# Four reorderings in a one-core decoder layer: query and key tiles by weight unit, the first branch's banks, the block sums, and the turns of the last rows

## The chip, the core and the metric

The kernel runs on one core of one Trainium2 chip. The metric is the time on the device in microseconds (us) of one execution; "the time" of a kernel is the median of its runs, while the profile and the trace come from one further, profiled execution. The engines are called by their names in the profile: PE (TensorE, with its weight loads apart as PEld), DVE (VectorE), ACT (ScalarE), POOL (GpSimd) and SP (SyncE, which issues most DMAs).

## The reference

One layer of a decoder, for 1024 tokens of width 1024, in float32:

```
xn   = rms_norm(x)
proj = xn @ w_in          # q, six key/value parts, 24 gates, conv in, memory q, 3 merge gates
A = sparse attention: compressed blocks, top-16 selected blocks, window of 512, each gated
B = GLU -> depthwise conv (31) -> layer_norm -> silu
C = attention over 256 memory tokens
merged = sig(g0) * (A @ w_nsa_out) + sig(g1) * (B @ w_conv_out) + sig(g2) * (C @ w_mem_out)
h   = x + merged @ w_out
out = h + (silu(hn @ w_gate) * (hn @ w_up)) @ w_down,   hn = rms_norm(h), d_ff = 2816
```

## The kernel before

**Products.** Each float32 operand is split in a high and a low part (`split`, L142: an ACT cast makes the high part at L143, a subtraction on DVE or POOL at L136 makes the low one). A product is three matmuls: high by high, high by low, low by high (`mm3`, L169; the matmuls are those of L162). A weight tile of 512 input rows and 256 columns is a *unit* (`unit`, L275); a product over 1024 input rows needs two units, u = 0 and u = 1, with four steps k of 128 rows each. `tok_proj` (L311) makes a tile of 256 tokens by 256 columns, token tile by token tile, and in each over all eight k, so over both units.

**Banks.** Results are summed in eight PSUM banks. Seven have the names ps0, ps1 and ps2 (three, three and one of them) and are taken in a fixed rotation by `bank`; with `at` a caller names the group. The eighth, pf, belongs to the *filler*; `fbank` takes it, and `anybank` takes it at every eighth call.

**Order.** The program text isn't the order of the engines' instructions. A scheduler lays each engine's instructions out ahead of time by priorities (the place in the text, plus an addition for work marked `low`) and by its own estimate of when operands are ready; `tc.add_manual_dep` ties one instruction behind another. On the chip each engine then runs its list strictly in order. Work marked `low(FILL)` is the filler (L825 to L839): the merge gates, 24 weight tiles with two halves each, so 48 products of 24 matmuls of 128x512. Each is summed in pf, copied by ACT to a tile fz (L838) and sent to memory (zd). It fills TensorE where the main work waits; all but the first 12 weight tiles are also tied along the attention, step by step.

**The stages.**
- To 346 us: norms and turns of x, the convolution and memory branches up to their projections, compressed keys.
- 346 to 371: the last query tiles (L603 to L614): eight token tiles of 280 columns, one after the other, each over both units; behind each, ACT copies, sigmoid and squares and a sum on DVE.
- 371 to 388: the LayerNorm of the convolution branch (L636 to L650): two sums over channels on TensorE, subtractions on DVE (L641), squares on ACT (L643).
- 388 to 456: keys and values (L660 to L684). For each of two weight pairs s, four tiles of 256 tokens; a finished key tile is normed, split and turned (`keys`, L668).
- 456 to 880: attention, along which the filler runs.
- 880 to 977: the three branches' output projections (L891 to L933): loop n_ over branches, dp over pairs of channel tiles, d_ and half inside; one tile is 12 matmuls. The gate comes back from zd, ACT makes its sigmoid (L903), and DVE multiplies it with the product: for the first branch directly into the sum `acc` (L914), for the others to a tile (L916) that is then added (POOL for the second, DVE at L917 for the third).
- 977 to 1062: h = x + merged @ w_out by seven block products (`out_product`, L1045, matmuls at L1052) of sums and differences of blocks of `merged`; four of these block sums for each j are made in place by `a_sums` (L883), called in the loop of the third branch at dp > 1. The sum of h is L1059, its squares L1061.
- 1040 to 1096: norm and turn of h in four groups of 256 rows. `scaled_h` (L980) takes the root (ACT, L154) and its reciprocal (DVE) and scales the rows (DVE, L986); `norm_h` (L989) turns them on TensorE (L1002) into four banks, splits them, and for the seven-product feed-forward part keeps copies (L1016) and differences. Between the turns of the last two groups stands `plain(0, 0)` (L965): the gate product and the up product of the first 128 columns, 24 matmuls each, with a Silu on ACT (L968) and a product on DVE (L970).
- From 1096: feed-forward and down projection, then the output.

Of the kernel before, what the change touches and what calls it, by code (L numbers as in the profile page):

```python
# [17 lines left out]
P = 128  # L18
# [15 lines left out]
ORDER = mybir.DependencyInfo(mybir.DependencyClass.NoSync, mybir.DependencyReason.DATA)  # L34
N_EARLY = 12
WB, LAG, SPREAD = 6, 4, 97
TAP_LEAD = 24
# [4 lines left out]
def hybrid_layer_kernel(  # L42
# [252 lines left out]
    def row_units(w, c0, alloc=wslab, eng=None, ready=None):  # L295
        return [unit(w[u * 512:(u + 1) * 512, c0:c0 + 256].rearrange("(k p) c -> p k c", p=P), [4, 256], alloc, eng,
                     ready=ready) for u in range(2)]

    def chan_proj(w, half, act=xn, n=P, alloc=bank):
# [292 lines left out]
    for u in range(2):  # L592
# [8 lines left out]
        ws.append(w)  # L601
    sums.append(small(NT * 4))
    for t in range(NT):  # L603
        half, a = t // 4, (t % 4) * P
        o = bank([WCOLS])
        for k in range(KT):
            w = ws[k // 4]
            mm3(o, xn(0, k, half, a, a + P), xn(1, k, half, a, a + P), w[:, 0, k % 4], w[:, 1, k % 4], k == 0,
                k == KT - 1)
# [4 lines left out]
        nc.vector.tensor_reduce(sums[-1][:, 4 * t:4 * t + 4], q.rearrange("p (h d) -> p h d", h=4), axis=AX.X, op=OP.add)  # L614
# [47 lines left out]
    for s, K, V in ((0, KS, VS), (1, KW, VW)):  # L662
# [8 lines left out]

        last = None
        for tp in range(4):
            v = tok_proj(ws, tp).rearrange("p t (a g d) -> p t a g d", a=2, g=2)
            kn = t2([2, 2, 64])
# [149 lines left out]
    with low(FILL):  # L825
        for n_ in range(3 * KT):
# [3 lines left out]
            for h_ in range(2):  # L830
# [7 lines left out]
                nc.scalar.copy(z, ps)  # L838
                nc.sync.dma_start(zd[b_, d_, :, h_ * 512:(h_ + 1) * 512], z)  # L839


# [40 lines left out]

    def a_sums(j):  # L883
        plus = nc.vector.tensor_tensor
        a11, a12, a21, a22 = (merged(th, kh, j) for th in range(2) for kh in range(2))
        plus(a22, a21, a22, op=OP.add)
        sub(nc.vector, a21, a11, a21)
        sub(nc.vector, a11, a22, a11)
        sub(nc.vector, a12, a12, a11)

    branches = ((1, ud, w_conv_out), (2, md, w_mem_out), (0, od, w_nsa_out))  # L891
    nxt = [unit(ud[k], [S], alloc=slab) for k in range(4)]
    for n_, (br, src, wt) in enumerate(branches):
        ins = nxt
        for dp in (range(4) if n_ < 2 else (0, 2, 1, 3)):
# [3 lines left out]
            for d_ in (2 * dp, 2 * dp + 1):  # L899
# [4 lines left out]
                for half in range(2):  # L904
                    z = zz[:, half * 512:(half + 1) * 512]
                    ps = anybank([512])
                    for k in range(4):
                        i_ = ins[k]
                        mm3(ps, w[:, 0, k, wc:wc + P], w[:, 1, k, wc:wc + P],
                            i_[:, 0, half * 512:(half + 1) * 512], i_[:, 1, half * 512:(half + 1) * 512],  # L910
                            k == 0, k == 3)
                    a = acc[dp][:, d_ % 2, half * 512:(half + 1) * 512]
# [5 lines left out]
                    if n_ == 2 and (half, dp // 2) != (1, 0):  # L918
# [4 lines left out]
                        split(m[:, 0, d_ % 2, :], m[:, 1, d_ % 2, :], a)  # L923
            if n_ == 2 and dp > 1:
                a_sums(dp - 2)
            if n_ == 2 and dp == 1:
# [37 lines left out]

    def plain(f, half, w):  # L965
        pg = chan_proj(w[0], half, alloc=anybank)
        s_ = t2([512])
        nc.scalar.activation(s_, pg, AF.Silu)  # L968
        pu = chan_proj(w[1], half, alloc=anybank)
        nc.vector.tensor_tensor(s_, pu, s_, op=OP.mult)  # L970
        emit_act(f, half, s_)
        return s_

    T = [[None] * 2 for _ in range(4)]
    raw, held = [None, None], [[], []]

# [12 lines left out]
    def norm_h(tp, js, at=None):  # L989
# [7 lines left out]
        def turned(kp):  # L997
            b = fbank([2, 256]) if at and kp == 3 else bank([2, 256], at=at and at[kp])
            for kk in range(2):
                k = 2 * kp + kk  # L1000
                for tt in range(2):
                    nc.tensor.transpose(b[:, kk, tt * P:(tt + 1) * P], js[tt][:, k * P:(k + 1) * P], ident)  # L1002
            split(XN[half][kp][:, 0, :, c], XN[half][kp][:, 1, :, c], b)
# [9 lines left out]
        if half == 0:  # L1013
            raw[0], raw[1] = [sb_fz() for _ in range(2)], t4([2, 2, 256])
            for kp in range(4):
                nc.scalar.copy(raw[0][kp] if kp < 2 else raw[1][:, kp - 2], turned(kp))  # L1016
            return
# [93 lines left out]
    finish(2, s_3, w_7, 1)  # L1111
    norm_h(0, js, (1, 1, 1))
    js = scaled_h(1)
    finish(2, left[1, 1], w_4, 0)
    nc.sync.dma_start(hd[2], H[2])
    js2 = scaled_h(2)
    norm_h(1, js, (1, 1, 1))
    w0 = gate_up(0)
    finish(3, s_3, w_7, 1)
    norm_h(2, js2, (0, 0, 1))  # L1120
    finish(3, left[1, 1], w_4, 0)
    nc.sync.dma_start(hd[3], H[3])
    js3 = scaled_h(3)
    for f_ in held[0]:
        f_()
    held[0].clear()
    a0 = plain(0, 0, w0)
    norm_h(3, js3)
    left_low(0, a0, plain(0, 1, w0))


# [212 lines left out]
```

## Time and profile before

| | us |
|---|---|
| median of 3 runs | 1705.43 (1704.92, 1705.43, 1708.69) |
| profiled execution | 1706.4 |
| its span in the trace | 1704.7 |
| PE busy | 1674.9 |
| DVE busy | 1056.9 |
| ACT busy | 786.6 |
| POOL busy | 558.0 |

The span goes from the first to the last instruction; the execution's time has 1.7 us more around it. The trace lists for each engine what it ran and, in brackets, how long it stood idle before and what ended that. A group "x24" is 24 instructions of one line and shape with nothing else between them; its duration includes their overlap. [...]

### The profile page before, as it was taken

Reading aid. Unit: us, or ns where it says so; the run is one execution under the profiler, and the core shown is the slowest. Engines: PE = TensorE matmul, PEld = TensorE weight load, DVE = VectorE, ACT = ScalarE, POOL = GpSimd, SP = SyncE. Lnnn points to the kernel's source line nnn. Section 1 sums busy time; section 2 is a strip of 40 time slices with the busy share of each in tenths; the row PEclk is TensorE's granted clock in tenths of the full one; section 3 lists DMA queues with packets and bytes.
Section 4 is the critical chain, followed back from the end, with each engine's and each line's share of the span. In section 5 each row is a group of like instructions: output and inputs, shape, how many; then the busy total and the mean of one; then the engine's idle time right before and its main releaser. Section 6 shows DMA issues by size and latency. Waiting matters only on the chain. (4 is left out here: it accounts for less than half of the span.)

```text
span 1704.7 us, 23845 instructions
## 1 busy us (share of the span) xinstructions
PE 1674.9 (98%) x8746; PEld 1427.5 (84%) x8746; DVE 1056.9 (62%) x1784; ACT 786.6 (46%) x1427; POOL 558.0 (33%) x531
## 2 busy tenths in 40 slices
PE   7999999999999999999999999999999999999998
PEld 7888899889888888888887878788888888888887
DVE  5398898735356566666654688764545455466664
ACT  6423554444477666676644346533222222233332
POOL 1110112314254434343115210565656776310000
PEclk9999999999999999999999999999999999999999
DMA  6445444222142232122466573233233545793763
GB/s 195 105 94 145 139 124 112 69 77 81 50 99 66 75 78 75 47 65 69 152 238 192 156 213 125 93 104 113 87 111 112 168 145 180 273 388 130 233 235 113
DMA packets 180448, 226.95 MB, mean 133 GB/s; under 512 B 11414, under 2 KB 118088, under 8 KB 179306
## 3 DMA queue, kind: packets, MB, share of 16 engines
q1 hardware_dynamic: 173850, 203.92, 36.2%
q0 software_dynamic: 6480, 21.50, 6.8%
q8 instruction: 69, 1.13, 0.3%
q14 instruction: 49, 0.40, 0.1%
HBM read 153.55 MB, written 50.33 MB: 120 GB/s over the span
## 5 line engine op out<-in xcount | busy, mean ns | idle before, releaser
L162 PE MATMUL ps<-slab,wsl 128*128 128x512 f32 (+1 forms) x1616 | 358.6, 380 | 0.0
L162 PEld LDWEIGHTS ps<-slab,wsl 128*128 128x128 f32 x1616 | 293.7, 188 | 58.0
L162 PE MATMUL pf<-slab,fsl 128*128 128x512 f32 x1236 | 327.3, 400 | 3.0 <-ACT fz L838 3.0
L162 PEld LDWEIGHTS pf<-slab,fsl 128*128 128x128 f32 x1236 | 224.9, 189 | 45.4 <-ACT fz L838 4.7
L162 PE MATMUL ps<-wsl,slab 128*128 128x256 f32 (+1 forms) x1344 | 175.6, 287 | 1.6 <-ACT slab L231 0.8
L162 PEld LDWEIGHTS ps<-wsl,slab 128*128 128x128 f32 x1344 | 169.2, 192 | 4.8 <-ACT slab L231 1.2
L1176 DVE TENSOR_TENSOR t<-ps,t 128x512 f32<-128x512 f32 x127 | 86.9, 688 | 121.0 <-PE ps L162 120.1
L162 PE MATMUL ps<-slab,fsl 128*128 128x512 f32 x684 | 159.6, 389 | 0.0
L408 DVE SCALAR_TENSOR_TENSOR slab<-slab,cw 128x1021 f32<-128x1021 f32 (+16 forms) x120 | 155.7, 1303 | 1.9
L162 PEld LDWEIGHTS ps<-slab,fsl 128*128 128x128 f32 x684 | 128.3, 188 | 26.6
L136 DVE TENSOR_TENSOR t<-ps,t 128x512 fp32r<-128x512 f32 (+2 forms) x175 | 118.4, 685 | 25.0 <-ACT t L143 23.6
L1278 PE MATMUL ps<-wsl 128*128 128x512 f32 x492 | 117.7, 389 | 0.0
L143 ACT CAST t<-ps 128x512 fp32r<-128x512 f32 (+1 forms) x172 | 96.3, 583 | 38.5 <-PE ps L782 30.5
L162 PE MATMUL ps<-t,slab 128*128 128x512 f32 (+1 forms) x360 | 110.1, 379 | 0.1
L1278 PEld LDWEIGHTS ps<-wsl 128*128 128x128 f32 x492 | 92.3, 188 | 19.2
L143 ACT CAST wsl<-st 128x1024 fp32r<-128x1024 f32 x64 | 67.3, 1052 | 78.5 <-PE ps L162 35.4
L162 PE MATMUL ps<-slab,qt 128*128 128x384 f32 (+3 forms) x384 | 97.0, 343 | 1.3 <-DVE sm L725 1.3
L143 ACT CAST wsl<-t 128x1024 fp32r<-128x1024 f32 (+2 forms) x50 | 48.2, 970 | 98.4 <-POOL t L136 31.9
L698 POOL TENSOR_SCALAR wsl<-wsl,sm,gsb 128x640 f32<-128x640 f32 (+7 forms) x76 | 58.8, 784 | 105.9 <-DVE sm L693 89.9
L136 DVE TENSOR_TENSOR wsl<-st,wsl 128x1024 fp32r<-128x1024 f32 x50 | 67.7, 1356 | 29.8 <-ACT wsl L143 29.0
L1278 PE MATMUL ps<-fsl 128*128 128x512 f32 x333 | 80.5, 389 | 0.0
L1189 POOL TENSOR_TENSOR t<-t,t 128x512 f32<-128x512 f32 x21 | 40.2, 1912 | 118.6 <-DVE t L1176 55.4
(256 smaller groups left out, 2831.6 us busy)
## 6 DMA issues: line engine op xcount, KB each, us to landing
t<-in_w_down_dram SPq DMA_DIRECT2D x70, 256.0 KB, 3.6
fst<-in_w_in_dram SPq DMA_DIRECT2D x24, 512.0 KB, 3.9
zd<-fz SPq DMA_DIRECT2D x48, 256.0 KB, 2.0
t<-zd SPq DMA_DIRECT2D x24, 512.0 KB, 5.3
st<-in_w_in_dram SPq DMA_DIRECT2D x22, 512.0 KB, 4.4
st<-in_w_gate_dram SPq DMA_DIRECT2D x22, 512.0 KB, 3.8
st<-in_w_up_dram SPq DMA_DIRECT2D x22, 512.0 KB, 4.0
ad<-t SPq DMA_DIRECT2D x44, 256.0 KB, 2.3
```

The source lines that it names most:

```text
L136: return eng.tensor_tensor(o, a, b, op=OP.subtract)
L143: first = nc.scalar.copy(hi, src)
L162: m = nc.tensor.matmul(o, a, b, start=start, stop=stop)
L408: return nc.vector.scalar_tensor_tensor(acc[:, s:], u[:, :S - s], cw[:, ct, 30 - s:31 - s], acc[:, s:], op0=OP.mult, op1=OP.add)
L698: nc.gpsimd.tensor_scalar(tiles[h], tiles[h], rec[:, h:h + 1], gsb[:, i, c0:c0 + 1], op0=OP.mult, op1=OP.mult)
L1176: nc.vector.tensor_tensor(o, a_, b_, op=OP.add)
L1189: nc.gpsimd.tensor_tensor(u4, u4, c22, op=OP.mult)
L1278: nc.tensor.matmul(B[t], a_, b_, start=start and k == 0 and j == 0, stop=k == FH - 1 and j == 2, skip_group_check=True)
```

## The change

Five edits, in the order of the program:

1. **Query and key tiles by unit.** A new `by_units` takes several tiles and runs the unit in the outer loop: unit 0 for all tiles, then unit 1. The last three query tiles go together so, and the last two key/value tiles (tp 2 and 3) of each weight pair.
2. **The first branch off the filler's bank.** For n_ = 0 the tiles take `bank` instead of `anybank`; the tile d_ = 1, half 0 is tied behind the last filler product.
3. **Block sums where used.** `a_sums` is cut in three, called ahead of the three `a_parts` that need them, instead of in the loop of the third branch.
4. **Last rows.** The turns of the last row group move into the up product of `plain(0, 0)`, ahead of its k = 5, and all four take ps banks (groups 0, 1, 0, 1) instead of what the rotation gives.
5. **Root and copies.** The third group's copies are made in the order 0, 2, 1, 3, and the last two are tied behind the last rows' root.

The core of the diff:

```diff
+    def by_units(ws, tiles, act=xn):
+        for u, w in enumerate(ws):
+            for o, t, first in tiles:
+                half, a = t // 4, (t % 4) * P
+                for k in range(4 * u, 4 * u + 4):
+                    ah, al = act(0, k, half, a, a + P), act(1, k, half, a, a + P)
+                    for j, (x_, hl) in enumerate(((ah, 0), (ah, 1), (al, 0))):
+                        m = nc.tensor.matmul(o, x_, w[:, hl, k % 4, :], start=first and k == 0 and j == 0,
+                                             stop=k == KT - 1 and j == 2, skip_group_check=True)
...
     for t in range(NT):
-        o = bank([WCOLS])
...
+        if t < 5:
+            outs.append(bank([WCOLS]))
+            by_units(ws, [(outs[t], t, True)])
+        elif t == 5:
+            outs += [bank([WCOLS]) for _ in range(3)]
+            by_units(ws, [(outs[t_], t_, True) for t_ in range(5, NT)])
+        o = outs[t]
...
-            v = tok_proj(ws, tp).rearrange("p t (a g d) -> p t a g d", a=2, g=2)
+            if tp < 2:
+                vs[tp] = tok_proj(ws, tp)
+            elif tp == 2:
+                for t_ in (2, 3):
+                    vs[t_] = bank([2, 256])
+                by_units(ws, [(vs[t_][:, tt, :], 2 * t_ + tt, tt == 0) for t_ in (2, 3) for tt in range(2)])
...
+    filled = products[-1][0]
...
-                    ps = anybank([512])
+                    ps = (anybank if n_ else bank)([512])
...
+                        if (n_, d_, half, k) == (0, FILLED, 0, 0):
+                            tc.add_manual_dep(m.ins, filled.name, ORDER, reason="behind the gates' products")
...
-            if n_ == 2 and dp > 1:
-                a_sums(dp - 2)
...
-    def plain(f, half, w):
+    def plain(f, half, w, between=None):
...
-        pu = chan_proj(w[1], half, alloc=anybank)
+        pu = anybank([512])
+        for k in range(KT):
+            ahead_ = between() if k == 5 and between else None
+            m = mm3(pu, w[1][:, 0, k, :], w[1][:, 1, k, :], xn(0, k, half), xn(1, k, half), k == 0, k == KT - 1)
+            behind(m, ahead_, "behind the last rows' turns")
...
-            for kp in range(4):
-                nc.scalar.copy(raw[0][kp] if kp < 2 else raw[1][:, kp - 2], turned(kp))
+            del copies[:]
+            for kp in (0, 2, 1, 3):
+                copies.append(nc.scalar.copy(raw[0][kp] if kp < 2 else raw[1][:, kp - 2], turned(kp)).ins)
...
+    a_sums(1)
     s_1 = a_parts(1, 1)
...
+    a_sums(2)
     s_2 = a_parts(0, 0)
...
+    a_sums(3)
     s_4 = a_parts(0, 1)
...
-    norm_h(3, js3)
+    for m in copies[2:]:
+        tc.add_manual_dep(m, roots[-1].name, ORDER, reason="behind the last rows' root")
+
+    def last_rows():
+        for f_ in held[0]:
+            f_()
+        held[0].clear()
+        norm_h(3, js3, (0, 1, 0, 1))
+        return turns[-4:]
+
+    a0 = plain(0, 0, w0, last_rows)
```

The compiled order of TensorE between the LayerNorm's sums and the keys, before (pf are filler tiles, ps_3142 and ps_3152 the variance sums, ps_3184 the first key/value tile):

```order
600 L162 MATMUL pf_7630<-slab_176,fsl_7626 128x512 x6
601 L162 MATMUL pf_7630<-slab_177,fsl_7626 128x512 x6
602 L162 MATMUL pf_7658<-slab_392,fsl_7626 128x512 x6
603 L162 MATMUL pf_7658<-slab_393,fsl_7626 128x512 x6
604 L162 MATMUL pf_7658<-slab_394,fsl_7626 128x512 x6
605 L162 MATMUL pf_7658<-slab_395,fsl_7626 128x512 x6
606 L162 MATMUL ps_3142<-slab_642,t_387_3118 128x512
607 L162 MATMUL ps_3152<-slab_642,t_387_3118 128x512
608 L162 MATMUL ps_3184<-wsl_3176,slab_174 128x256 x6
```

The same place in the changed order (ps_3321 is the key/value tile tp = 3, wsl_3176 and wsl_3181 its two units; two token tiles of two rows of six matmuls each):

```order
600 L163 MATMUL pf_7630<-slab_176,fsl_7626 128x512 x6
601 L163 MATMUL pf_7630<-slab_177,fsl_7626 128x512 x6
602 L307 MATMUL ps_3321<-wsl_3176,slab_392 128x256 x6
603 L307 MATMUL ps_3321<-wsl_3176,slab_393 128x256 x6
604 L307 MATMUL ps_3321<-wsl_3176,slab_392 128x256 x6
605 L307 MATMUL ps_3321<-wsl_3176,slab_393 128x256 x6
606 L307 MATMUL ps_3321<-wsl_3181,slab_394 128x256 x6
607 L307 MATMUL ps_3321<-wsl_3181,slab_395 128x256 x6
608 L307 MATMUL ps_3321<-wsl_3181,slab_394 128x256 x6
609 L307 MATMUL ps_3321<-wsl_3181,slab_395 128x256 x6
610 L163 MATMUL pf_7658<-slab_392,fsl_7626 128x512 x6
```

48 matmuls of a key/value tile now stand between two filler tiles that followed each other.

TensorE at the last rows' turns, before (ps_10407 is the gate product, ps_10434 the up product, t_1772 and t_1773 the two scaled tiles of the last rows):

```order
2086 L162 MATMUL ps_10407<-slab_10146,wsl_10285 128x512 x5
2087 L162 MATMUL ps_10434<-slab_10146,fsl_10290 128x512 x5
2088 L1002 MATMUL ps_10461<-ident,t_1772_10391 128x128
2089 L1002 MATMUL ps_10468<-ident,t_1772_10391 128x128
2090 L1002 MATMUL ps_10500<-ident,t_1772_10391 128x128
2091 L1002 MATMUL ps_10461<-ident,t_1773_10392 128x128
...
2100 L1002 MATMUL ps_10493<-ident,t_1772_10391 128x128
2101 L1002 MATMUL ps_10493<-ident,t_1773_10392 128x128
```

And in the changed order (ps_10395 is the gate product, ps_10422 the up product):

```order
2077 L163 MATMUL ps_10422<-slab_10145,fsl_10290 128x512 x3
2078 L163 MATMUL ps_10395<-slab_10146,wsl_10285 128x512 x6
2079 L1031 MATMUL ps_10450<-ident,t_1772_10391 128x128
2080 L1031 MATMUL ps_10457<-ident,t_1772_10391 128x128
2081 L1031 MATMUL ps_10482<-ident,t_1772_10391 128x128
2082 L1031 MATMUL ps_10489<-ident,t_1772_10391 128x128
2083 L1031 MATMUL ps_10450<-ident,t_1773_10392 128x128
...
2094 L1031 MATMUL ps_10489<-ident,t_1773_10392 128x128
2095 L163 MATMUL ps_10422<-slab_10145,fsl_10290 128x512 x3
2096 L163 MATMUL ps_10422<-slab_10146,fsl_10290 128x512 x6
```

The turns stand ahead of the last nine matmuls of the up product, and all on banks of their own.

VectorE at the block sums for j = 0 in the third branch, before (the rows of 128x2x512 are the four sums; slab_8740 to slab_8743 hold `merged`):

```order
1221 L886 TENSOR_TENSOR slab_8742<-slab_8740,slab_8742 128x2x512
1222 L916 TENSOR_TENSOR t_1647_9522<-ps_9543,t_1647_9522 128x512
1223 L136 TENSOR_TENSOR slab_8740<-slab_8740 128x2x512
1224 L136 TENSOR_TENSOR slab_9540<-slab_8741,slab_9540 128x512
1225 L917 TENSOR_TENSOR slab_8741<-slab_8741,t_1647_9522 128x512
1226 L136 TENSOR_TENSOR slab_8740<-slab_8742,slab_8740 128x2x512
1227 L916 TENSOR_TENSOR t_1651_9558<-ps_9561,t_1651_9558 128x512
1228 L136 TENSOR_TENSOR slab_8742<-slab_8742,slab_8740 128x2x512
```

And in the changed order, whose L909, L137, L943 and L944 are the L886, L136, L916 and L917 of before:

```order
1221 L909 TENSOR_TENSOR slab_8742<-slab_8740,slab_8742 128x2x512
1222 L943 TENSOR_TENSOR t_1647_9518<-ps_9539,t_1647_9518 128x512
1223 L137 TENSOR_TENSOR slab_8740<-slab_8740 128x2x512
1224 L137 TENSOR_TENSOR slab_9536<-slab_8741,slab_9536 128x512
1225 L944 TENSOR_TENSOR slab_8741<-slab_8741,t_1647_9518 128x512
1226 L137 TENSOR_TENSOR slab_8740<-slab_8742,slab_8740 128x2x512
1227 L943 TENSOR_TENSOR t_1651_9554<-ps_9557,t_1651_9554 128x512
1228 L137 TENSOR_TENSOR slab_8742<-slab_8742,slab_8740 128x2x512
```

Nothing has moved here: the sums stand at the same rows, among the same merges.

More of the change, by code (lines that the diff above doesn't have):

```diff
@@ L35 @@
 N_EARLY = 12
+FILLED = 1
 WB, LAG, SPREAD = 6, 4, 97
@@ L602, in hybrid_layer_kernel @@
     sums.append(small(NT * 4))
+    outs = []
     for t in range(NT):
-        half, a = t // 4, (t % 4) * P
-        o = bank([WCOLS])
[L606 to L609, printed above, removed]
+        if t < 5:
[5 more added lines that the diff above has]
+        o = outs[t]
         q = o[:, :256]
@@ L672, in hybrid_layer_kernel @@
         last = None
+        vs = {}
         for tp in range(4):
-            v = tok_proj(ws, tp).rearrange("p t (a g d) -> p t a g d", a=2, g=2)
+            if tp < 2:
[4 more added lines that the diff above has]
+                by_units(ws, [(vs[t_][:, tt, :], 2 * t_ + tt, tt == 0) for t_ in (2, 3) for tt in range(2)])
+            v = vs[tp].rearrange("p t (a g d) -> p t a g d", a=2, g=2)
             kn = t2([2, 2, 64])
@@ L881, in a_parts, with a_sums @@
         return a
[L883 to L889, printed above, removed]
+    def a_sums(n):
+        for j in range(2):
+            a11, a12, a21, a22 = (merged(th, kh, j) for th in range(2) for kh in range(2))
+            if n == 1:
+                nc.vector.tensor_tensor(a22, a21, a22, op=OP.add)
+            elif n == 2:
+                sub(nc.vector, a21, a11, a21)
+                sub(nc.vector, a11, a22, a11)
+            else:
+                sub(nc.vector, a12, a12, a11)
     branches = ((1, ud, w_conv_out), (2, md, w_mem_out), (0, od, w_nsa_out))
@@ L905, in hybrid_layer_kernel @@
                     z = zz[:, half * 512:(half + 1) * 512]
-                    ps = anybank([512])
+                    ps = (anybank if n_ else bank)([512])
                     for k in range(4):
                         i_ = ins[k]
-                        mm3(ps, w[:, 0, k, wc:wc + P], w[:, 1, k, wc:wc + P],
-                            i_[:, 0, half * 512:(half + 1) * 512], i_[:, 1, half * 512:(half + 1) * 512],
-                            k == 0, k == 3)
+                        m = mm3(ps, w[:, 0, k, wc:wc + P], w[:, 1, k, wc:wc + P],
+                                i_[:, 0, half * 512:(half + 1) * 512], i_[:, 1, half * 512:(half + 1) * 512],
+                                k == 0, k == 3)
+                        if (n_, d_, half, k) == (0, FILLED, 0, 0):
+                            tc.add_manual_dep(m.ins, filled.name, ORDER, reason="behind the gates' products")
                     a = acc[dp][:, d_ % 2, half * 512:(half + 1) * 512]
@@ L974, in hybrid_layer_kernel @@
     T = [[None] * 2 for _ in range(4)]
-    raw, held = [None, None], [[], []]
+    raw, held, copies, turns = [None, None], [[], []], [], []
     def sb_fz():
@@ L997, in turned @@
         def turned(kp):
-            b = fbank([2, 256]) if at and kp == 3 else bank([2, 256], at=at and at[kp])
+            b = fbank([2, 256]) if at and at[kp] is None else bank([2, 256], at=at and at[kp])
             for kk in range(2):
@@ L1001, in turned @@
                 for tt in range(2):
-                    nc.tensor.transpose(b[:, kk, tt * P:(tt + 1) * P], js[tt][:, k * P:(k + 1) * P], ident)
+                    turns.append(nc.tensor.transpose(b[:, kk, tt * P:(tt + 1) * P], js[tt][:, k * P:(k + 1) * P],
+                                                     ident).ins)
             split(XN[half][kp][:, 0, :, c], XN[half][kp][:, 1, :, c], b)
@@ L1111, in hybrid_layer_kernel @@
     finish(2, s_3, w_7, 1)
-    norm_h(0, js, (1, 1, 1))
+    norm_h(0, js, (1, 1, 1, None))
     js = scaled_h(1)
@@ L1116, in hybrid_layer_kernel @@
     js2 = scaled_h(2)
-    norm_h(1, js, (1, 1, 1))
+    norm_h(1, js, (1, 1, 1, None))
     w0 = gate_up(0)
     finish(3, s_3, w_7, 1)
-    norm_h(2, js2, (0, 0, 1))
+    norm_h(2, js2, (0, 0, 1, None))
     finish(3, left[1, 1], w_4, 0)
@@ L1123, in hybrid_layer_kernel @@
     js3 = scaled_h(3)
[L1124 to L1127, printed above, removed]
-    norm_h(3, js3)
+    for m in copies[2:]:
[7 more added lines that the diff above has]
+    a0 = plain(0, 0, w0, last_rows)
     left_low(0, a0, plain(0, 1, w0))
```

1 line of the change is left out of this document (added).

## The prediction

> **What bounds the kernel now.** The page's busy times come first.
>
> ```profile
> span 1704.7 us, 23845 instructions
> ...
> PE 1674.9 (98%) x8746; PEld 1427.5 (84%) x8746; DVE 1056.9 (62%) x1784; ACT 786.6 (46%) x1427; POOL 558.0 (33%) x531
> ```
>
> TensorE stands still for 1704.7 - 1674.9 = 29.8 us in all, and the change takes no matmul away. So it can win only TensorE's idle time, and whatever that idle time does to the clock. TensorE's waits, grouped by what ended them, give the places (time in total, times, longest):
>
> ```profile
> PE pf L162 <- ACT fz L838: 3.7, 4, 1.8
> PE ps L1052 <- DVE t L916: 3.5, 2, 2.9
> PE ps L1002 <- DVE t L970: 2.2, 1, 2.2
> ...
> PE ps L162 <- DVE sm L725: 1.3, 1, 1.3
> ```
>
> The first three are what the change speaks of: the filler bank, the block product behind the third branch, and the turns of the last rows. The windows of those stretches (length; busy time and instructions of PE, PEld, DVE, ACT, POOL; granted clock; DMA) show the second cost:
>
> ```profile
> 380.00:390.00 10.00, 9.97 (x37) 7.47 (x38) 8.13 (x4) 3.51 (x5) 7.00 (x3) 0.83 0.14 52
> 966.50:987.40 20.90, 17.36 (x73) 13.72 (x72) 20.73 (x25) 9.68 (x16) 11.25 (x9) 0.96 0.71 184
> 985.00:990.00 5.00, 3.83 (x11) 3.08 (x12) 4.28 (x6) 2.74 (x6) 3.04 (x3) 0.66 1.03 424
> ```
>
> Right behind two of the gaps the granted clock falls to a mean of 0.83 and 0.66: 10.00 x 0.17 = 1.7 us and 5.00 x 0.34 = 1.7 us of clock lost, as far as TensorE had work in it.
>
> **Query and key tiles: -3.6 us.** TensorE's timeline from the end of the projections (start, duration, group, idle time before it and what ended it):
>
> ```profile
> 372.18 6.05 PE L162 MATMUL pf<-slab,fsl 128*128 128x512 f32 x24
> 380.03 7.36 PE L162 MATMUL pf<-slab,fsl 128*128 128x512 f32 x24 [1.81 <-ACT fz L838]
> 387.23 1.88 PE L162 MATMUL ps<-slab,t 128*128 128x512 f32 x4
> 388.55 17.83 PE L162 MATMUL ps<-wsl,slab 128*128 128x256 f32 x144
> ...
> 443.89 5.74 PE L162 MATMUL pf<-slab,fsl 128*128 128x512 f32 x24 [0.68 <-ACT fz L838]
> ```
>
> Two filler tiles stand back to back in the one filler bank. The second waits 1.81 us for the copy that empties the bank, then its 24 matmuls take 7.36 us where the same 24 take 5.74 at 443.89: 1.62 us for the clock. Why the copy is late stands on ScalarE and VectorE:
>
> ```profile
> 376.56 2.95 ACT L643 ACTIVATE slab<-slab 128x1024 f32<-128x1024 f32 x3 [0.42 <-DVE slab L641]
> 379.42 0.56 ACT L838 COPY fz<-pf 128x512 f32<-128x512 f32 x1
> ```
> ```profile
> 374.32 1.22 DVE L136 TENSOR_TENSOR wsl<-st,wsl 128x1024 fp32r<-128x1024 f32 x1
> 375.45 0.41 DVE L614 TENSOR_REDUCE smw<-ps 128x4 f32<-128x256 f32 x1
> 375.79 2.47 DVE L641 TENSOR_TENSOR slab<-slab,ps 128x512 f32<-128x512 f32 x4
> ```
>
> Three squares of 0.98 us each stand ahead of the copy. In the changed order 48 key/value matmuls lie between the two filler tiles. At 17.83 / 144 = 0.124 us each they last 5.94 us, from about 377.7 (380.03 - 1.81 - 0.56, when the first filler's last matmul starts and drains) to 383.7; the copy is done by 379.42 + 0.56 = 379.98. So the 1.81 goes with 3.7 us to spare, and with the gap the 1.62. Both halves of those weights are ready in time: the second one's low part ends at 374.32 + 1.22 = 375.54. What could be late next is the key tile's own bank, if the subtractions of L641 still hold it: they end at 375.79 + 2.47 = 378.26, and TensorE arrives at about 377.7. I charge 0.3 us, between 0 and 0.6. The 0.68 at 443.89 is the same pattern; in the changed order eight turns stand there between two filler tiles, which hide most of it: -0.5, between 0 and -0.68. Nothing else is cheaper or dearer by units: the same matmuls, other order; the three query banks are freed together 36 matmuls later, but the next tiles have a bank of their own. Sum: -1.81 - 1.62 - 0.5 + 0.3 = -3.6.
>
> [...]
>
> **First branch: -1.5 us.**
>
> ```profile
> 899.62 1.75 PE L162 MATMUL pf<-slab,fsl 128*128 128x512 f32 x7
> 902.04 3.02 PE L162 MATMUL pf<-slab,wsl 128*128 128x512 f32 x12 [0.68 <-ACT fz L838]
> 905.84 2.37 PE L162 MATMUL pf<-slab,wsl 128*128 128x512 f32 x9 [0.79 <-DVE slab L914]
> ```
>
> Filler, branch tile, branch tile, all in the filler bank, each waiting for the reader of the one before: 0.68 + 0.79 = 1.47. With `bank` these two tiles take other banks, and by the order they stand further ahead, among the filler; no two tiles of the filler bank follow each other there any more. The last filler product is now followed by a tile in a free bank. Between -1.47 and, if the tiles' gates come late from memory for the earlier place, 0. I take -1.5, since the rows show two plain bank waits.
>
> **Block sums: 0.** The block product waits here:
>
> ```profile
> 978.18 3.70 PE L1052 MATMUL ps<-wsl,slab 128*128 128x512 f32 x15 [0.60 <-DVE t L916]
> 981.72 1.52 PE L1052 MATMUL ps<-fsl,slab 128*128 128x512 f32 x6
> 986.17 2.93 PE L1052 MATMUL ps<-wsl,slab 128*128 128x512 f32 x6 [2.93 <-DVE t L916]
> ```
> ```profile
> 967.71 1.22 DVE L886 TENSOR_TENSOR slab<-slab,slab 128x1024 f32<-128x1024 f32 x1
> ```
>
> VectorE is busy for 20.73 of the 20.90 us from 966.5 to 987.4, and four block sums of at least 1.22 us (L886 and three subtractions) stand among the merges that free the banks. If they moved behind the merges, up to 4.9 us of VectorE would clear the way, and the 0.60 + 2.93 with 2.93 - 1.52 = 1.4 of clock would go. But in the compiled order they do not move: VectorE's rows there are the same before and after. So this part says one thing and does another, and I cost it at 0. The stage can still shift: if TensorE arrives earlier and VectorE does not, the gap grows by up to the 1.5 of the first branch; if the half-speed window does not come, 1.4 is won. Bounds -4.9 to +1.5.
>
> **Last rows: -1.5 us.**
>
> ```profile
> 1074.66 0.49 PE L1002 MATMUL ps<-ident,t 128*128 128x128 f32 x3
> 1075.92 1.20 PE L1002 MATMUL ps<-ident,t 128*128 128x128 f32 x9 [0.77 <-DVE t L986]
> 1079.34 0.66 PE L1002 MATMUL ps<-ident,t 128*128 128x128 f32 x4 [2.21 <-DVE t L970]
> ```
> ```profile
> 1068.83 0.59 ACT L1016 COPY fz<-ps 128x512 f32<-128x512 f32 x1 [1.39 <-POOL t L136]
> ...
> 1070.83 0.21 ACT L154 ACTIVATE sm<-sm 128x2 f32<-128x2 f32 x1
> ```
> ```profile
> 1071.78 4.09 DVE L986 SCALAR_TENSOR_TENSOR t<-slab,sm,gff 128x1024 f32<-128x1024 f32 x2
> ```
> ```profile
> 1070.01 8.21 POOL L136 TENSOR_TENSOR slab<-t,slab 128x512 fp32r<-128x512 f32 x5
> ```
>
> The 2.21 is a bank held until the up product is multiplied (L970). All sixteen turns now have banks that don't wait for that, so it goes. The turns also move ahead of the up product's last 9 matmuls, 9 x 0.24 (5.74 / 24, the filler's row) = 2.2 us, so TensorE arrives at 1074.66 - 2.2 = 1072.5. The rows they turn come from the two scalings L986, done at 1071.78 + 4.09 = 1075.87, the first about 1073.8. If these stay, TensorE waits 1.3 for the first and, after four turns of 0.16 (0.49 / 3), 1.4 for the second: 2.7 against 0.77 + 2.21 = 2.98, a gain of 0.3. But the root at 1070.83, on which the scalings hang, gets earlier: the copy at 1068.83, which had waited for GpSimd, is now behind it. What stays ahead of it is a cast of a difference that GpSimd makes, behind two keeps now. The copy's 0.49 and the cast at 1070.36 bound the shift: I take 0.9 earlier, between 0 and 1.6 (the wait of 1.39 gone too). Then the second rows are there at 1075.0, the waits are 0.4 + 1.5, and the gain 2.98 - 1.9 = 1.1. The scalings lie beside GpSimd's keeps (8.21 / 5 = 1.64 each); with fewer of them beside, the pair gets shorter than 4.09 too, and all the 2.98 could go. From 0 to -3.0, I take -1.5, a little over the worked 1.1 for that. Behind the turns nothing of the feed-forward part waits on them at present.
>
> [...]
>
> **Attention: 0.** The scheduler puts the filler along the attention anew, since 22 filler matmuls more have run before it. TensorE has one wait of 1.3 us there (L725). It may go, or another like it come: -1.3 to +1.8, with no row that favours either.
>
> **Sum.** -3.6 - 1.5 + 0 - 1.5 + 0 = -6.6. The profiled execution of before took 1706.4 us, 1.7 over its span, and 1.0 over the median of 1705.43. So 1706.4 - 6.6 = 1699.8 profiled, and 1705.43 - 6.6 = 1698.8 for the median, say **1698.8 us**.
>
> **Rivals.**
> *The gains run into VectorE* (0.16). The 966 to 987 stretch is VectorE's, so what TensorE wins at 902 comes back as a longer gap at 986 (+1.5), and the last rows' scalings don't come earlier (+1.3). For it: 20.73 of 20.90 busy. Against it: VectorE's own stretch begins with tiles that TensorE feeds. 1698.8 + 2.8 = 1701.6.
> *The half-speed windows have nothing to do with the gaps* (0.07). Then the 1.62 behind 380 stays: 1700.4. [...] Against it: 0.83 and 0.66 come right behind two of the longest gaps, and the other windows shown do not fall.
> *The block product loses its gap* (0.13). Its tiles come a little otherwise upstream, the wait gets shorter than the one that trips the clock: up to 2.9 + 1.4 = 4.3 more, 1694.5.
> *Slower: the attention starves of filler* (0.06). The filler hides the softmax chain; 22 matmuls of it, 22 x 0.24 = 5.3 us, are spent before. If the turn-by-turn order leaves waits uncovered, each costs like the one at 380: 1.81 + 1.62 = 3.4. Two make up the 6.6 all but for nothing; from the third on it is slower, 1698.8 + 3 x 3.4 = 1709.0. Against it: the filler's later part is tied to the attention step by step, and the order comes together again with that of before.
> One such gap alone (0.10) gives 1702.2. The forecast itself keeps 0.48.
>
> **Range and chances.** A measurement here tells about 0.2% from no change, 3.4 us: faster is below 1702.0. The forecast, the clock rival, the shorter block product and most of the first rival lie below it; the one-gap case and the rest of the first lie within; the starved attention above. That gives 0.78 faster, 0.16 same, 0.06 slower. The range takes the forecast's bounds and the neighbours, 1693.5 to 1704.0.
>
> **What would show it.** Right: no filler wait near 380 and no granted clock below 1 in 380 to 390; no wait for L838 or L914 at 900; the gap before L1052 about as it was, near 3; the last turns with waits of 1 to 2 us in all and none for L970. Wrong: new TensorE waits of over 1 us between 450 and 640, a longer wait for the merges at 980, or a wait for L986's successor of near 3 us.

## The result, and the profile after

The changed kernel takes 1698.05 us (median of 6 runs, 1694.33 to 1700.75), beside 1706.56 for the kernel before on the same chip: ratio 0.9946, 95% interval 0.9931 to 0.9962, so -9.2 us, between -6.5 and -11.8; the medians differ by 8.5. The prediction had 1698.8 and -6.6. The profiled execution, the slowest of the six, took 1700.75, with a span of 1698.9:

```profile
span 1698.9 us, 23848 instructions
...
PE 1674.5 (99%) x8746; PEld 1427.8 (84%) x8746; DVE 1053.8 (62%) x1784; ACT 786.1 (46%) x1427; POOL 557.4 (33%) x531
```

TensorE's idle time has gone from 29.8 to 1698.9 - 1674.5 = 24.4 us. Its waits, grouped as in the list of before (L1083 is the old L1052, L859 the old L838, L1031 the turns, L1015 the scaling):

```profile
PE ps L1083 <- DVE t L943: 4.7, 2, 2.6
...
PE pf L163 <- ACT fz L859: 1.8, 2, 1.3
...
PE ps L1031 <- DVE t L1015: 0.7, 1, 0.7
```

The filler bank costs 1.8 instead of 3.7, the turns 0.7 instead of 2.2 + 0.8, and the wait for L970 is gone. The block product costs more, 4.7 instead of 3.5.

The *granted clock* is the profile's figure for TensorE's clock: 1.00 is full speed, 0.50 half. In what follows a *half-speed window* is a stretch of 3.41 us in which it is 0.50; from the first stretch at full speed to TensorE's last matmul the trace of before has half speed at 381.42 and 985.58, for 3.41 us each, and that of the change at 460.22 for 3.41 and at 975.64 for 6.83. If TensorE has work all through such a window, I estimate its cost as 3.41 x 0.5 = 1.7 us; the 24 filler matmuls at 380.03 in the trace of before took 7.36 us with a window, those at 443.89 without one 5.74, so 1.62 less.

**Query and keys.** TensorE's timeline where the 1.81 stood:

```profile
370.97 6.04 PE L163 MATMUL pf<-slab,fsl 128*128 128x512 f32 x24
377.10 6.02 PE L307 MATMUL ps<-wsl,slab 128*128 128x256 f32 x48
382.96 5.63 PE L163 MATMUL pf<-slab,fsl 128*128 128x512 f32 x24
388.43 1.88 PE L163 MATMUL ps<-slab,t 128*128 128x512 f32 x4
```

No wait is left, and the second filler tile takes 5.63 us. From the first tile's start to the variance sums it is 17.46 us with 5.86 of key matmuls inside (382.96 - 377.10), so 11.60 for what took 387.23 - 372.18 = 15.05: -3.45 us.

**First branch.** The last filler product is followed by a tile in another bank, and the next tile in the filler's bank begins without a wait:

```profile
898.83 1.52 PE L163 MATMUL ps<-slab,wsl 128*128 128x512 f32 x6
900.19 2.88 PE L163 MATMUL pf<-slab,wsl 128*128 128x512 f32 x12
```

**The spent filler** (the 22 filler matmuls that have run earlier) is missed a little later, at the first turns of the attention:

```profile
457.53 0.44 PE L163 MATMUL ps<-slab,qt 128*128 128x128 f32 x2 [0.22 <-DVE sm L746]
457.81 0.62 PE L729 MATMUL ps<-ident,t 128*128 128x128 f32 x4
459.71 6.89 PE L163 MATMUL pf<-slab,fsl 128*128 128x512 f32 x22 [1.28 <-ACT fz L859]
```

The windows (as above: length, busy times, granted clock, DMA) show what followed this wait and the block product's:

```profile
455.00:460.00 5.00, 3.50 (x24) 2.83 (x23) 0.66 (x8) 2.87 (x9) 0.00 (x0) 1.00 0.00 0
460.00:465.00 5.00, 5.00 (x16) 3.93 (x16) 1.77 (x10) 3.86 (x12) 3.26 (x7) 0.66 0.14 52
970.00:975.00 5.00, 2.03 (x8) 1.05 (x6) 5.00 (x6) 0.00 (x0) 2.63 (x3) 1.00 0.56 106
975.00:980.00 5.00, 3.22 (x8) 2.54 (x9) 4.92 (x7) 1.24 (x2) 3.22 (x2) 0.56 0.92 258
980.00:985.00 5.00, 5.00 (x17) 3.71 (x16) 4.92 (x9) 3.86 (x7) 0.00 (x0) 0.75 1.02 416
```

One half-speed window at 460, two at the block product. TensorE and VectorE there:

```profile
973.24 0.96 PE L1083 MATMUL ps<-wsl,slab 128*128 128x512 f32 x3 [2.17 <-DVE t L943]
976.78 6.33 PE L1083 MATMUL ps<-wsl,slab 128*128 128x512 f32 x15 [2.57 <-DVE t L943]
982.95 1.53 PE L1083 MATMUL ps<-fsl,slab 128*128 128x512 f32 x6
```
```profile
964.49 0.69 DVE L944 TENSOR_TENSOR slab<-slab,t 128x512 f32<-128x512 f32 x1
965.10 1.22 DVE L909 TENSOR_TENSOR slab<-slab,slab 128x1024 f32<-128x1024 f32 x1
966.23 0.68 DVE L943 TENSOR_TENSOR t<-ps,t 128x512 f32<-128x512 f32 x1
```

The block sum L909 still stands between the merges L944 and L943. The 15 matmuls at 976.78 take 6.33 us, where they took 3.70 before.

**Last rows.** TensorE, then ScalarE, then VectorE:

```profile
1069.65 0.60 PE L1031 MATMUL ps<-ident,t 128*128 128x128 f32 x4
1070.92 1.53 PE L1031 MATMUL ps<-ident,t 128*128 128x128 f32 x12 [0.68 <-DVE t L1015]
1072.20 2.32 PE L163 MATMUL ps<-slab,fsl 128*128 128x512 f32 x9
```
```profile
1065.86 0.20 ACT L155 ACTIVATE sm<-sm 128x2 f32<-128x2 f32 x1 [0.41 <-DVE sm L1011]
1065.96 0.57 ACT L1047 COPY fz<-ps 128x512 f32<-128x512 f32 x1
```
```profile
1066.29 4.57 DVE L1015 SCALAR_TENSOR_TENSOR t<-slab,sm,gff 128x1024 f32<-128x1024 f32 x2
```

The root now waits for its own sum alone, and the copies come behind it.

Where the profiled 5.8 us came from, by the start of the matmul with the same number in both traces. Up to each of these numbers both kernels have run equally many matmuls of every shape, but for two at the first third of the attention (384 columns wide after, 512 before, about 0.1 us):

| place | before | after | shift | change since the row above |
|---|---|---|---|---|
| before the last queries | 316.62 | 315.47 | -1.15 | nothing changed yet: the start |
| first third of the attention | 605.79 | 602.17 | -3.62 | -2.47 |
| end of the attention | 825.29 | 821.83 | -3.46 | +0.16 |
| first branch | 906.18 | 900.42 | -5.76 | -2.30 |
| third branch | 962.68 | 956.86 | -5.82 | -0.06 |
| block products | 1036.12 | 1033.10 | -3.02 | +2.80 |
| feed-forward part | 1304.27 | 1298.93 | -5.34 | -2.32 |

The -1.15 of the first row is no gain of the change: at this place the twelve traces of this study lie between 314.73 and 317.18. Up to the first third of the attention 3.45, the 0.68 at 443.89 and the 1.26 of the wait for L725 (at 550 before, gone after) are won, and 0.22, 1.28 and a half-speed window of some 1.5 are paid.

### The profile page after: what moved, and what is told of

The parts are those of the page before. It is cut to its first block, busy times and chain, and to the rows that moved or that the text cites. A ratio compares the mean times of both kernels' runs of the same rounds, so it can differ in the third digit from the quotient of the medians.

```text
span 1698.9 us, 23848 instructions
## 1 busy us (share of the span) xinstructions
PE 1674.5 (99%) x8746; PEld 1427.8 (84%) x8746; DVE 1053.8 (62%) x1784; ACT 786.1 (46%) x1427; POOL 557.4 (33%) x531
## 4 chain that ended last, share of the span: by engine, by line
PE 68%; DVE 4%; DMA 4%; issue 2%; ACT 2%; POOL 1%; SPq 0%; ACTq 0%; POOLq 0%
PE ps L163 31%; PE pf L163 14%; PE ps L1318 11%; PE ps L803 3%; PE ps L307 3%; PE ps L1083 3%; PE pf L1318 1%; DMA t<-zd 1%; DVE slab L137 1%; DVE t L1015 1%; DMA st<-od 1%; POOL slab L944 0%; DMA st<-md 0%; ACT slab L144 0%; PE ps L790 0%
## 5 line engine op out<-in xcount | busy, mean ns | idle before, releaser
L163 PE MATMUL ps<-slab,wsl 128*128 128x512 f32 (+1 forms) x1640 | 364.1, 381 | 0.0
L163 PEld LDWEIGHTS ps<-slab,wsl 128*128 128x128 f32 x1640 | 298.1, 188 | 59.1 <-DVE slab L137 0.3
L137 DVE TENSOR_TENSOR t<-ps,t 128x512 fp32r<-128x512 f32 (+2 forms) x175 | 118.3, 685 | 27.3 <-ACT t L144 25.6
L163 PE MATMUL ps<-wsl,slab 128*128 128x256 f32 x960 | 125.4, 285 | 1.4 <-ACT slab L232 0.7
L163 PEld LDWEIGHTS ps<-wsl,slab 128*128 128x128 f32 x960 | 120.0, 191 | 4.0 <-ACT slab L232 1.1
L137 DVE TENSOR_TENSOR wsl<-st,wsl 128x1024 fp32r<-128x1024 f32 x50 | 64.9, 1300 | 41.4 <-ACT wsl L144 40.5
```

What stands on the lines that cost most here:

```text
L137: return eng.tensor_tensor(o, a, b, op=OP.subtract)
L163: m = nc.tensor.matmul(o, a, b, start=start, stop=stop)
```

## The experiments

Ratios are to the kernel before on the same chip. The ten kernels came in three groups, each beside its own runs of the kernel before.

**The query and key tiles alone** (`by_units` and its two callers):

```diff
+            by_units(ws, [(outs[t_], t_, True) for t_ in range(5, NT)])
...
+                by_units(ws, [(vs[t_][:, tt, :], 2 * t_ + tt, tt == 0) for t_ in (2, 3) for tt in range(2)])
```

> The kernel before with the query and key tiles by unit, and nothing else. Theory A (each edit wins the idle time at its own place): the 1.81 us wait at 380 and the half-speed window behind it (1.6) go, the 0.68 at 444 goes; the filler spent there leaves a wait of about 1.3 us at the first turns of the attention, with or without a half-speed window (1.6) behind it. Sum -2.5 to -4 us against the kernel before, ratio about 0.998. Theory B (what TensorE wins ahead of 966 comes back as a longer wait at the block product, since the third branch's gates arrive at their own pace): the waits at 380 go just the same, but the waits at the block product grow from 3.5 to 5 us or more, and the whole is within 1.5 us of before.

Measured 0.9980 (0.9970 to 0.9990), 1705.20 against 1708.70: -3.5 us, as theory A has it. The waits at the block product are 4.3 us in this trace, against 3.5 before; unchanged orders vary by more, as the control shows. The wait of 1.28 is there at 459.75 in this trace too, but no half-speed window behind it:

```profile
455.00:460.00 5.00, 3.50 (x24) 2.83 (x23) 0.67 (x8) 2.82 (x9) 0.00 (x0) 1.00 0.00 0
460.00:465.00 5.00, 5.00 (x24) 4.12 (x24) 1.77 (x10) 3.91 (x12) 3.27 (x7) 1.00 0.14 52
```

The same busy time ahead, 3.50 of 5.00, and a granted clock of 0.66 in the one execution, 1.00 in the other. Six traces of this study have this wait of 1.28; five have a half-speed window behind it, one of them two.

**The first branch alone** (the bank, and the tie behind the last filler product):

```diff
-                    ps = anybank([512])
+                    ps = (anybank if n_ else bank)([512])
...
+                        if (n_, d_, half, k) == (0, FILLED, 0, 0):
+                            tc.add_manual_dep(m.ins, filled.name, ORDER, reason="behind the gates' products")
```

> The kernel before with the first branch's tiles off the filler's bank, and nothing else. Theory A: the waits of 0.68 and 0.79 at 902 and 906 go and nothing comes back: -1.5 to -2 us, waits at the block product still 3.5. Theory B: the same two waits go, but the two waits at the block product together grow by as much, from 3.5 to about 5, and the whole is -0.5 to +1 us, more if a second half-speed window (1.7) is set off there.

Measured 0.9988 (0.9979 to 0.9997): -2.1 us, theory A's size, though the profiled execution has theory B's longer waits (5.5 at the block product). One trace can't settle that; more follow below. It showed something else at 380, where nothing is changed:

```profile
378.27 5.74 PE L163 MATMUL pf<-slab,fsl 128*128 128x512 f32 x24 [1.81 <-ACT fz L839]
385.36 1.98 PE L163 MATMUL ps<-slab,t 128*128 128x512 f32 x4 [1.35 <-POOL slab L632]
```

Behind the same 1.81 the clock stayed at full speed, the filler took 5.74 us, and TensorE then waited 1.35 us for GpSimd's sums. From 372.18 to 387.23 it had been 15.05 us with the half-speed window; here it is 385.36 - 370.41 = 14.95, the first tile having started at 370.41. So at this place the slow clock cost nothing; it only filled a wait. The trace of the last rows alone (next) has the same 1.81 and 1.35, and full speed.

**The last rows alone** (root, copies, turns and Silu):

```diff
+            ahead_ = between() if k == 5 and between else None
...
+        tc.add_manual_dep(m, roots[-1].name, ORDER, reason="behind the last rows' root")
```

> The kernel before with the last rows' root, turns and Silu in fixed order, and nothing else. Both theories: the waits of 0.77 and 2.21 at 1076 and 1079 shrink to one of about 0.7, everything ahead of 1040 stays as before, and nothing waits behind it: -2.3 us. If the root did not get earlier, the waits would be 2.7 us together and the whole would be -0.3.

Measured 0.9969 (0.9958 to 0.9980), 1703.78 against 1708.70: by the ratio -5.3 us, more than the 2.3 that both theories had. The trace has the expected wait, and one only:

```profile
1073.53 0.60 PE L1006 MATMUL ps<-ident,t 128*128 128x128 f32 x4
1074.82 1.42 PE L1006 MATMUL ps<-ident,t 128*128 128x128 f32 x11 [0.70 <-DVE t L990]
```

From 1060 to 1304 in the trace of before (the matmuls with the same two numbers in both) this trace needs 241.46 us and that of before 243.84: -2.4. On the rest see the control.

**The control: the block sums alone**, called where they are used:

```diff
-            if n_ == 2 and dp > 1:
-                a_sums(dp - 2)
...
+    a_sums(1)
```

> The kernel before with the block sums called where they are used, and nothing else. The compiled order of every engine is the same as before, so both theories give no difference: ratio 1.000, with its interval over 1. A difference here would be the size of what the chip varies by itself.

Measured 1.0000 (0.9990 to 1.0009). This part does nothing, as the compiled order said. The trace is another execution of the order of before, and it differs from the first where waits are long. At the last rows the waits are the same, but here the clock fell behind them:

```profile
1078.70 1.20 PE L1003 MATMUL ps<-ident,t 128*128 128x128 f32 x9 [0.79 <-DVE t L987]
1082.12 1.00 PE L1003 MATMUL ps<-ident,t 128*128 128x128 f32 x4 [2.22 <-DVE t L971]
```
```profile
1080.00:1087.00 7.00, 4.88 (x17) 4.04 (x18) 5.63 (x9) 4.52 (x8) 6.20 (x5) 0.76 0.10 37
```

The same stretch took 245.45 us here, 1.6 more than in the first trace. In the profile of the first branch alone two half-speed windows follow these waits (granted clock 0.77 from 1073 to 1080, 0.74 from 1080 to 1087), and it took 247.09, 3.25 more. In the profile of before there had been none (1.00 from 1080 to 1087). So the last rows' waits cost 3 us in one execution and up to 3 + 3.25 in another. That is part of what was missing from the -5.3, but not shown to be all of it: of the five traces with the old order of these rows three have no window here (243.8 us each), so the five average 244.8, and the gain by them is 3.3, at the edge of the interval (3.4 to 7.2). The waits at the block product are 5.0 us in the control (1.60 + 3.41) against 3.5, with the order unchanged.

**The block sums really moved**, on top of the change:

```diff
+            for m in ms:
+                tc.add_manual_dep(m.ins, merges[-1].name, ORDER, reason="behind the last merge")
```

> The changed kernel with the block sums really moved: each is tied behind the last merge of the third branch on VectorE. Theory A (VectorE's block sums among the merges hold the banks that the block product waits for): the waits at the block product fall from 4.7 us to under 1.5, the half-speed windows there (1.7 each) go, and the time falls by 3 to 6 us against the changed kernel, ratio to the kernel before about 0.991. Theory B (the merges wait for the gates that come through memory, the sums only fill that time): the waits stay at 3.5 to 5 us and the time within 1 us of the changed kernel's.

Measured 0.9917 (0.9904 to 0.9931), 1694.99: 4 to 5 us under the changed kernel (0.9946, and 0.9940 when it was measured again, below). Theory A holds. TensorE's block product, and the end of VectorE's merges:

```profile
972.05 4.24 PE L1085 MATMUL ps<-wsl,slab 128*128 128x512 f32 x18
976.13 1.29 PE L1085 MATMUL ps<-fsl,slab 128*128 128x512 f32 x5
977.27 1.52 PE L1085 MATMUL ps<-wsl,slab 128*128 128x512 f32 x6
```
```profile
976.82 0.69 DVE L137 TENSOR_TENSOR slab<-slab,slab 128x512 fp32r<-128x512 f32 x1
977.43 0.68 DVE L946 TENSOR_TENSOR slab<-slab,t 128x512 f32<-128x512 f32 x1
978.03 1.22 DVE L909 TENSOR_TENSOR slab<-slab,slab 128x1024 f32<-128x1024 f32 x1
```

The first block sum (L909) comes behind the last merge (L946); nothing waits at the product but 0.4 us later on. The third branch to the block products took 68.7 us instead of 76.2. The four traces with moved sums need 68.7 to 69.9 there, the eight others 72.9 to 76.5.

**The same on the kernel before**, without the rest of the change:

> The kernel before with nothing but the block sums tied behind the last merge of the third branch. Theory A (the sums on VectorE hold the banks, whatever stands ahead): the waits at the block product fall from about 3.5 to under 1 us and no half-speed window (1.7) follows them, so -4 to -5 us against before, ratio about 0.997. Theory B (the sums hold the banks only when TensorE has been made faster ahead of them): -1 us or less.

Measured 0.9971 (0.9958 to 0.9983): -5 us, waits of 0.21 and 0.76. Theory A: the sums hold the banks whatever stands ahead.

**The moved sums without the first branch's edit:**

> The changed kernel with the block sums really moved, but the first branch's tiles back on the filler's bank. In the run of the first-branch edit alone the waits at the block product grew to 5.5 us, so the edit's gain was lost there. Theory A (it was lost only because VectorE's sums held the banks): here the waits of 0.68 and 0.79 near 897 cost their full 1.5 to 2 us, so the ratio to the kernel before is about 0.9928, against 0.9917 with the edit. Theory B (the merges take up whatever is won ahead of them, sums or not): the ratio is 0.9917 as with the edit, and the wait at the block product is near zero in both.

Measured 0.9928 (0.9915 to 0.9942), against 0.9917 with the edit. Here the two waits of the filler bank are back:

```profile
900.85 3.02 PE L162 MATMUL pf<-slab,wsl 128*128 128x512 f32 x12 [0.68 <-ACT fz L858]
904.65 3.04 PE L162 MATMUL pf<-slab,wsl 128*128 128x512 f32 x12 [0.78 <-DVE slab L939]
```

**The change without the first branch's edit, and the change again**, side by side:

> The changed kernel with the first branch's tiles back on the filler's bank, block sums among the merges as the scheduler put them. Theory A (what the first branch wins stays won, here too): the waits of 0.68 and 0.79 are back and cost their 1.5 to 2 us, so the ratio to the kernel before is 0.0009 to 0.0012 above that of the changed kernel beside it. Theory B (it is lost in the block product's wait): the two waits are back, the block product's waits are 1 to 2 us shorter than in the changed kernel, and both ratios agree within 0.0004.

> The changed kernel as it is, for the comparison on the same chip: ratio 0.9946 as before, half-speed windows in other places or numbers than in its first profile, since the waits that set them off (1.3 us at 459, two of over 2 us at the block product) fall differently against the clock's own time from run to run.

Measured 0.9956 (0.9943 to 0.9968) without it and 0.9940 (0.9923 to 0.9956) with it. The block product's waits in the two traces:

```profile
PE ps L1079 <- DVE t L939: 4.0, 2, 3.3
```
```profile
PE ps L1083 <- DVE t L943: 3.4, 1, 3.4
```

They are not shorter without the edit (4.0, against 3.4 here and 4.7 in the changed kernel's first trace). Three comparisons (alone, with the moved sums, with the sums as they were) give the edit 0.0012, 0.0011 and 0.0016, so 1.9 to 2.7 us. The intervals of the last two pairs overlap, and no comparison settles it by itself, but all three agree with theory A. The traces say the same: from the end of the attention to the first branch (825.29 to 906.18 in the table) the five with the edit need 78.6 to 79.0 us, the seven without 80.8 to 81.7. And with moved sums the way on to the block products costs 68.7 and 69.9 with the edit, 69.6 and 69.6 without, so theory B, that the merges take the gain back, isn't borne out. The half-speed windows of the changed kernel's second trace lie at 462.5 (one) and 981.3 (two): as many as in its first, behind the same waits, where the expectation had other places or numbers. Its reason, the clock's own time, was the author's estimate.

**The moved sums with the first exponentials behind the filler's copy:**

```diff
+    for m_ in exps[:4]:
+        tc.add_manual_dep(m_, fcopies[17].name, ORDER, reason="behind the filler copy")
```

> The changed kernel with the block sums really moved, and the first softmax's four exponentials tied behind the filler's copy that TensorE waits for at 459. Theory A: the wait of 1.28 us there shrinks to 0.5 to 0.7 and no half-speed window follows it: -0.7 to -1.5 us against the version without this tie, ratio to the kernel before about 0.991. Rival: the exponentials, 0.6 us later, open a wait of the same size at the next values, and nothing is won: 0.9917.

Measured 0.9907 (0.9893 to 0.9920) against 0.9917: not told apart. The wait of 1.28 is gone and no window follows, but a wait of 0.54 has come:

```profile
458.67 0.44 PE L163 MATMUL ps<-slab,qt 128*128 128x128 f32 x2 [0.22 <-DVE sm L746]
459.12 4.58 PE L163 MATMUL pf<-slab,fsl 128*128 128x512 f32 x19
...
467.31 0.44 PE L163 MATMUL ps<-slab,qt 128*128 128x128 f32 x2 [0.54 <-DVE sm L774]
```

From the place before the last queries to the first third of the attention it needs 285.40 us; the query and key tiles alone, with the 1.28 but without a window, needed 285.35, and the moved sums without the tie, with the 1.28 and a window, 286.97. The rival holds for the wait itself: what the tie can win is only the window, when there is one. This version and the one with the moved sums alone have the lowest ratios of the study, 0.0023 to 0.0039 under the changed kernel's two.

## Why the prediction was right, point by point

**The number.** That 1698.8 came within 0.8 us of 1698.05 is in part luck. The gain was 8.5 by the medians and 9.2 by the ratio, not 6.6; but the six runs of the kernel before have a median 1.1 above the 1705.43 of three runs that the prediction started from. The parts measured alone (0.9980, 0.9988, 1.0000 and 0.9969) multiply to 0.9937, against 0.9946 and 0.9940 for the whole: within the noise they add up. The mechanism, that TensorE wins its idle time at these places and the clock behind it, is borne out at the three places where the order moved, but for one cause (the 1.62, below). Two of the sizes were too small.

**Query and keys, -3.6:** -3.5 measured for this edit alone. At its place the -3.45 is the 1.81 + 1.62 of the prediction (the 0.3 for the key tile's bank wasn't needed: no wait stands at 377.10), but one term had the wrong cause: the 1.62 behind the gap was read as the price of the slow clock. Without the slow clock TensorE waits 1.35 for GpSimd there. By luck the key matmuls cover that wait too, so the sum stayed right. What the prediction left open, the attention with 22 matmuls less of filler, cost 0.22 + 1.28 and mostly a window, and the 1.26 for L725 and the 0.68 at 443.89 went: no rest to speak of.

**First branch, -1.5:** -1.9 to -2.7. The two waits are gone. Their idle time, 1.47, was a little less than their cost: in the rows of before, start to start, the 7 matmuls at 899.62 and the 12 at 902.04 take 2.42 and 3.80 us, where 19 in an unbroken run take 4.4 (60 in 13.76 us at 902.91 in the changed trace), so 1.8 are lost. A matmul of 128x512 that stands alone took 0.39 us (at 1074.36 in that trace), one in that run 13.76 / 60 = 0.23; with this overlap of 0.16 lost at each wait, an estimate, 1.47 + 2 x 0.16 is the 1.8. The rival that VectorE's stretch would take this back was tested three ways and isn't borne out. What the profiled pair showed as +2.80 at the block products is waits of 4.7 instead of 3.5 and a second window, and unchanged orders vary by as much there (3.5 and 5.0).

**Block sums, 0:** 1.0000 for the edit alone. The step from "the order is the same" to "no time" held. The other half of the step, what it would bring if it did what it says, was put at up to 4.9 us of VectorE's time and the waits with the clock; done by a dependency it brought 4 to 5 us.

**Last rows, -1.5:** this term was mis-sized; it measured -2.3 in the traces and -5.3 in the time. TensorE arrived 2.05 us earlier against its surroundings (1074.66 to 1069.65, with everything ahead shifted by 2.96), as worked out. But the root came 4.97 - 2.96 = 2.0 earlier, not 0.9, and not within the bound of 1.6: GpSimd's difference, thought to be still ahead of it, was there in time, since the casts had moved up too. So one wait of 0.7 is left, not 0.4 + 1.5. The allowance that the two scalings get shorter was wrong: they took 4.57 us, not less than 4.09. GpSimd, which stood idle beside the pairs of 2.47 and 2.55 at 1046.72 and 1052.75 in the trace of before, was at work beside them all the way (four keeps, 6.97 us from 1066.27). And the one profile of before had no half-speed window behind these waits, where two of the four other executions of that order have one or two; the term left that out. With these windows the traces give 3.3 of the 5.3; where the rest lies isn't shown.

**The signs.** Of those named for being right, most came: there is no filler wait near 380, the clock from 380 to 390 is 1.00, and the waits for L838 and L914 at 900 and for L970 are gone; the turns wait 0.7, a little less than the 1 to 2. Two of those named for being wrong did come: a new wait of over 1 us between 450 and 640 (the 1.28), and longer waits at the block product (4.7 together instead of 3.5, though unchanged orders have up to 5.0 there). So the case of one gap in the attention, which the prediction gave a chance of 0.10 and a price of 3.4, is what happened there, at 1.28 and up to 1.7; the 1.26 for L725 that went, and the larger gains of the first branch and the last rows, hid it in the total.

**The clock.** The mean granted clock tells how much the times owe to it at most. A window at half speed lowers the mean by 3.41 x 0.5 / 1700 = 0.001 and costs, by the estimate above, up to 1.7 us. (The mean also counts a stretch at half speed behind TensorE's last matmul, which ends at 1700.19 in the trace of before: from 1702.38 to the end at 1704.7, where TensorE has nothing to do.)

| kernel | runs | mean clock | mean time, us |
|---|---|---|---|
| before, beside the first four experiments | 24 | 0.9970 | 1708.8 |
| query and keys alone | 11 | 0.9977 | 1704.9 |
| first branch alone | 12 | 0.9968 | 1706.7 |
| last rows alone | 6 | 0.9983 | 1703.7 |
| the change | 6 | 0.9987 | 1697.8 |
| with moved sums | 5 | 0.9996 | 1694.8 |

By this an execution of the change holds 1.7 half-speed windows fewer, of at most 3.0, which is up to 2.9 us, beside the waits themselves (29.8 - 24.4 = 5.4, of which 0.1 falls ahead of the last queries: the 1.15 there is busy time for the rest): together 8.3 at most, of the 8.5 between the medians. The row of the change and that of before are from different groups of runs; for the change measured again, beside runs of before in its own group, it is 0.9980 against 0.9967, so 1.3 windows. The last rows alone have 1.3 windows fewer too. The prediction's -6.6 counted the windows of one execution.

## What to carry to other kernels

Here gaps of 1.3 to 3.4 us on TensorE cost themselves and, in some executions, one or two half-speed windows behind them; price such a gap over several executions, not by the one that was profiled. Before costing an edit of the program's text, see whether the compiled order moves: the block sums' edit was a no-op until a dependency forced it, and then it was worth as much as any other part. And where a slow stretch of TensorE precedes a wait for another engine, check what would be late next before booking the slow stretch as a gain.

## What the runs showed of the hardware

In the trace of before the first half-speed window begins at 381.42 and ends at 384.83, and the next begins at 985.58: 600.75 us after the first's end, 176.0 times the 3.413 us that a window lasts there. In the changed kernel's trace they begin at 460.22 and 975.64, so 515.41 us apart, 151.0 times 3.413. One and the same wait was followed by different clocks: behind the 1.28 us at 459 the granted clock from 460 to 465 was 0.66 in the change, and 1.00 in the query and key tiles alone. Stretches of 3.41 us around the 1.28, in the changed kernel:

```profile
456.81:460.22 3.41, 1.91 (x11) 1.32 (x11) 0.66 (x8) 3.09 (x10) 0.00 (x0) 1.00 0.00 0
460.22:463.64 3.42, 3.42 (x9) 2.67 (x9) 1.77 (x10) 3.42 (x10) 2.31 (x6) 0.50 0.20 77
```

And with the query and key tiles alone:

```profile
454.44:457.85 3.41, 3.19 (x21) 2.64 (x21) 0.67 (x8) 0.68 (x1) 0.00 (x0) 1.00 0.00 0
457.85:461.27 3.42, 2.14 (x13) 1.64 (x13) 0.72 (x6) 3.41 (x12) 0.00 (x0) 1.00 0.20 76
```

In the first the wait and the small matmuls ahead of it share one stretch, with TensorE busy for 1.91 us of it; in the second an edge parts them, and TensorE is busy for 3.19 and 2.14.

More such stretches, with TensorE's busy time in each:

| trace | stretch | granted clock | PE busy | granted clock in the next 3.41 us |
|---|---|---|---|---|
| before | 378.00:381.42, with the wait of 1.81 | 1.00 | 1.61 | 0.50 |
| before | 982.16:985.57, with most of the wait of 2.93 | 1.00 | 1.08 | 0.50 |
| before | 1077.74:1081.15, with most of the wait of 2.21 | 1.00 | 1.81 | 1.00 |
| the change | 456.81:460.22, with the wait of 1.28 | 1.00 | 1.91 | 0.50 |
| the change | 972.22:975.64, parts of the waits of 2.17 and 2.57 | 1.00 | 0.96 | 0.50 |
| before | 381.42:384.83 | 0.50 | 3.41 | 1.00 |
| before | 985.57:988.99 | 0.50 | 2.82 | 1.00 |
| the change | 460.22:463.64 | 0.50 | 3.42 | 1.00 |
| the change | 975.64:979.05 | 0.50 | 2.27 | 0.50 |
| the change | 979.05:982.46 | 0.50 | 3.41 | 1.00 |

In these rows neither the length of the wait nor TensorE's busy time alone tells what followed: 2.21 us of wait had full speed behind it and 1.28 had half, a busy time of 1.81 had full speed and 1.91 had half. What decides isn't shown.
